# Layer 1 attention: ten chunks of probabilities turned by DMA, their low parts on GpSimd, and a second score pass on 64 rows

## The chip, the cores and the metric

The kernel runs on one core of one Trainium2 chip. A core has five engines with an instruction queue each: TensorE (PE in the profile; PEld are its weight loads), VectorE (DVE), ScalarE (ACT), GpSimd (POOL) and SyncE (SP), which issues most DMAs. On-chip data lies in SBUF, 128 partitions wide; TensorE writes to PSUM, eight banks of 128 x 512 numbers of 4 bytes. The metric is the device time of one execution in microseconds, the median of several runs.

## The reference, cut to what matters

A two-layer transformer backbone without a channel mixer, on 1024 latent tokens and 256 context tokens of width 1024, in 32-bit floats. Layer 0 mixes with multi-head latent attention. Layer 1, where the change lies, mixes with differential attention: eight heads, each with two score maps of head size 64 and one set of values of size 128.

```python
q = q.reshape(bsz, n, B_HEADS, 2, B_HEAD)              # 8 heads, 2 maps, 64
k = k.reshape(bsz, n, B_HEADS, 2, B_HEAD)
v = v.reshape(bsz, n, B_HEADS, 2 * B_HEAD)             # 128 per head
o1 = softmax(q[..., 0, :] @ [k, k_c][..., 0, :].T * scale) @ [v, v_c]
o2 = softmax(q[..., 1, :] @ [k, k_c][..., 1, :].T * scale) @ [v, v_c]
o = o1 - lam_full * o2
o = rms_norm(o, g_sub) * (1.0 - lambda_init)
x = layer_norm(ALPHA * x + gate * ((o * silu(gate_in)) @ out_w), ln_g, ln_b)
```

Queries and keys of the latent tokens are turned by axial rotary tables before this. Every query sees 1024 latent keys and 256 context keys, 1280 = ten chunks of 128. Layer 1 gives out the latent tokens alone.

## The kernel before, in words

**Precision.** TensorE works on 16-bit floats here. A number that must be more exact is split into a high part (its 16-bit rounding) and a low part (the rest, again 16 bits), and a product becomes three matmuls: high by high, high by low, low by high (`mm3`, L217 to L220).

**A tile of attention.** Layer 1 goes over 8 heads x 8 query tiles of 128 tokens, 64 tiles, in `attend` (L1789). For each tile and each map `m`:

- Scores (`chunk`, `sc_`, L1854 to L1868). A map's keys lie in `KS{m}`: the high part of its 64 rows on partitions 0 to 63, the low part on 64 to 127. Its queries lie in `QS{m}`, the high part twice, and in `Q1{m}`, the low part twice. The first pass (L1855) is QS by KS, which gives high by high and high by low at once; the second (L1856) is Q1 by KS. So 512 columns take two matmuls of 128 rows. The 1024 latent keys of a map fill two banks of kind `p` (four exist), the context keys of both maps share the one bank `c`.
- Maxima (`maxima`, L1870) on VectorE: per bank, then `bound{m}`, the negative maximum per query (L1879).
- Exponentials (`exps`, L1882) on ScalarE, with the bound as bias and the sum as a second result, into `p0` or `p1` in SBUF, 128 x 1280 in 32 bits.
- Join (`join`, L1889) on VectorE: `p0 + p1 * (-lambda * sum0 / sum1)`, 128 x 1280 (L1897).
- Turning: the weighted sum needs the probabilities with keys on the partitions, so each 128 x 128 chunk is transposed. Chunks 0 to 7 (`far`, L1900): ScalarE writes the high part, scaled by a power of two `lcf[0]` (L1902), VectorE the low part (L1903), into `dd`, and one transposing DMA moves both to `pd` (L1905). Chunks 8 and 9, the context (`turns`, L1791): TensorE transposes them in 32 bits (L1798), ScalarE takes the high part `ph` (L1803) and VectorE the low part `pl` (L1805) out of the bank.
- Weighted sum (`values`, L1809): 30 matmuls of 128 columns (L1820 to L1822), chunks 8 and 9 first. Then ScalarE scales it out (L1826) and squares it (L1827), GpSimd normalises it (L193, L194, L1838), and SP stores it. The unscaling of `lcf[0]` sits in `vic`, with which `w.us` scales each head's factor (L1613).

The weighted sum of a tile is written into the next tile's list of work (`before`).

**Beside it.** While the tiles of head h run, the weights of the next head are loaded, scaled and split (`weights`), and its keys, queries and values are projected (`keys`, `queries`, `vals`). Projections are TensorE's filler between scores and weighted sums. Keys and queries go through a rope (ScalarE L1643, VectorE L1645 and L1646, GpSimd L1647 and L1648), are split (high part on ScalarE, low part on GpSimd, L1666 and L1692), and are moved by DMAs of 64 partitions to the layout above (`k.move`, `q.move`, issued at L118): four DMAs per key chunk, eight per query block. Beside head 7 the output projection of finished tiles takes the place of the next head's projections (`out_tile`, L1952), after the output weights are prepared (`out_raw`, `out_split`).

**What sets the order.** Head 0's projections are written out in line (`prod_k1`, `prod_q1`, `prod_v1`, `prod_w`), and `lambda_of` works out lambda and `lcf` during layer 0's output projection. The rest of layer 1 goes through a planner, `Plan` (L688): every step is a task with an engine, a cost in us, what it reads and writes, and a due time `at` (in tiles) to which `OFF` adds an offset by kind. `run` simulates the engines greedily, with the rings of buffers (`TAG1`, `TAGL`, `PSB`), the windows `EPS1` and `AHEAD`, and `PORT`, the kinds that may not overlap on VectorE and GpSimd. The result is a fixed order of instructions on each engine (`tc.manual_schedule`). SP's queue is one of them: a DMA whose data are not ready holds up those behind it.

Of the kernel before, what the change touches and what calls it, by code (L numbers as in the profile page):

```python
# [46 lines left out]
OFF = {"bound0": -12.4, "bound1": -23.45, "exp0": -3.35, "exp1": -5.5, "far.hi": -26.55, "far.lo": -9.05,
       "far.move": -2.85, "g.add": -0.7, "g.bias": -0.45, "g.keep": -9.05, "g.load": -0.2, "g.sum": -1.65, "g.zero":
       1.4, "join": -11.0, "k.ctx": -17.05, "k.hi": 2.85, "k.lo": -1.45, "k.move": -17.4, "late": -57.8, "max.c":
       -5.8, "max0": -14.2, "max1": -5.85, "o.ga": -9.6, "o.gb": 2.3, "o.hi": 0.65, "o.lo": -25.2, "o.mul": -0.9,  # L50
       "open": -22.75, "prod": 0.2, "pv": -13.1, "pv.gate": -10.4, "pv.norm": 3.2, "pv.out": -6.5, "pv.sq": -25.1,
       "pv.store": -25.15, "pv.us": -11.45, "q.hi": -11.65, "q.lo": -8.45, "q.move": -9.9, "r.add": -10.4, "r.cos":
       0.1, "r.out": -0.95, "r.sin": -28.4, "r.swap": 2.65, "score0": 0.4, "score1": 0.1, "scorec": -4.45, "sums":
       -26.05, "turn.hi0": -0.35, "turn.lo0": 0.95, "turn0": -7.95, "v.gate": -5.1, "v.hi": -13.6, "v.keep": 3.6,
       "v.lo": -3.6, "v.octx": -38.95, "v.out": 2.9, "v.pctx": -0.05, "v.prod": -0.4, "v.silu": 0.25, "v.store":
       3.75, "v.turn": -4.5, "w.hi": 0.2, "w.lo": 0.05, "w.load": -5.55, "w.root": 1.6, "w.scale": 3.75, "w.sq":
       2.35, "w.sum": -21.8, "w.unit": 0.5, "w.us": -32.05, "x.gate": -13.35, "x.hi": -14.55, "x.lo": 4.2, "x.load":
       3.6, "x.low": 5.5, "x.mul": 0.8, "z.add": -9.0, "z.agg": -5.6, "z.bn": 3.65, "z.end": 16.45, "z.g": -11.3,
# [18 lines left out]
KD = 8  # L77
# [8 lines left out]
def hybrid_kernel(  # L86
# [601 lines left out]
    class Plan:  # L688
# [3 lines left out]
        PORT |= {("G", k) for k in "r.sin r.add k.lo q.lo v.lo o.lo x.gate x.lo z.mul z.g2 z.g3 s.lo v.sub".split()}  # L692
# [545 lines left out]
    def lambda_of():  # L1238
# [218 lines left out]
    def prod_k1(h, made=()):  # L1457
# [680 lines left out]
```

## Time and profile before

| what | value |
|---|---|
| median of 3 runs | 1667.47 us (1666.78 to 1668.52) |
| profiled execution, its own time | 1667.77 us |
| span of its instructions | 1666.0 us |
| granted TensorE clock, mean | 0.990 |
| layer 1 attention, first scores to last weighted sum | 918 to 1646 us |
| DMA, mean over the span | 113 GB/s |

The page gives busy times per engine over the whole span; a busy TensorE is one whose pipelined matmuls overlap without a gap, so the time of one more matmul is read from start to start and not from its duration. Waiting is told for each group as the idle time of its engine just before it, with the instruction that ended it. Views by stretch, by waits, by group and along the timeline answer for shorter times than the whole span.

### The profile page before, as it was taken

The numbers are of one execution on the slowest core, as the hardware profiler recorded it, in microseconds if no ns is written. First come the engines' busy times: TensorE is split into PE (matmuls) and PEld (weight loads), VectorE is DVE, ScalarE is ACT, GpSimd is POOL, SyncE is SP. The second block draws the span as 40 slices with busy tenths as digits, with TensorE's granted clock in tenths as the row PEclk, the third lists the DMA queues.
The fourth block names the chain that finished last, engine by engine and source line by source line (L and its number), as shares of the span: only waits on it lengthen the run. The fifth ranks groups of instructions, "written<-read, shape, count | busy, mean of one in ns | idle before, by whom it ended". The sixth has DMA issues, their size and how long they took to land. (4 is left out here: it accounts for less than half of the span.)

```text
span 1666.0 us, 35966 instructions
## 1 busy us (share of the span) xinstructions
PE 1586.8 (95%) x14052; PEld 1176.6 (71%) x14052; DVE 1241.7 (75%) x1941; ACT 1132.0 (68%) x2164; POOL 918.2 (55%) x772
## 2 busy tenths in 40 slices
PE   7999999999999999989999999999999999996998
PEld 6999966566666666667777586757576757675776
DVE  7757856777676676746773799999898979897764
ACT  2652147777887888945454888787878787868542
POOL 1523026767777777854555354545464646467554
PEclk9999999999999999989999999999999999998999
DMA  9347620101111111355442356554645444556562
GB/s 320 92 133 233 208 81 21 42 23 50 42 56 48 37 36 42 101 168 182 153 149 80 88 115 143 127 131 105 140 90 143 112 101 104 122 137 182 137 173 76
DMA packets 249463, 188.36 MB, mean 113 GB/s; under 512 B 147559, under 2 KB 224967, under 8 KB 249294
## 3 DMA queue, kind: packets, MB, share of 16 engines
q1 hardware_dynamic: 241422, 178.73, 40.3%
q10 hardware_dynamic: 7872, 7.34, 1.3%
q8 instruction: 110, 1.80, 0.5%
q14 instruction: 59, 0.48, 0.1%
HBM read 98.65 MB, written 27.07 MB: 75 GB/s over the span
## 5 line engine op out<-in xcount | busy, mean ns | idle before, releaser
L989 POOL TENSOR_TENSOR pl<-p,ph 128x1024 f16<-128x1024 f32 (+1 forms) x176 | 364.6, 2091 | 108.9 <-ACT ph L987 67.9
L985 ACT ACTIVATE p<-ps_a,esc 128x1024 f32<-128x1024 f32 (+1 forms) x176 | 188.6, 1072 | 63.9 <-PE ps_a L981 59.5
L934 DVE TENSOR_REDUCE mx<-ps_a 128x1 f32<-128x1024 f32 x128 | 156.3, 1222 | 75.7 <-PE ps_a L930 75.2
L1884 ACT ACTIVATE p<-ps_p,mx 128x512 f32<-128x512 f32 x256 | 174.4, 688 | 46.7 <-DVE mx L1879 44.6
L987 ACT CAST ph<-p 128x1024 f16<-128x1024 f32 (+1 forms) x176 | 176.5, 1006 | 4.8
L1877 DVE TENSOR_REDUCE mx<-ps_p 128x1 f32<-128x512 f32 x256 | 165.5, 680 | 8.1 <-PE ps_p L1856 7.9
L979 PE MATMUL ps_a<-qH,KH 100*128 100x512 f16 x320 | 122.5, 383 | 0.2 <-ACT p L985 0.2
L980 PE MATMUL ps_a<-qH,KL 96*128 96x512 f16 x320 | 121.9, 381 | 0.0
L981 PE MATMUL ps_a<-qL,KH 96*128 96x512 f16 x320 | 121.0, 378 | 0.0
L1897 DVE SCALAR_TENSOR_TENSOR p<-p,sm,p 128x1280 f32<-128x1280 f32 x64 | 107.4, 1678 | 1.2
L997 PE MATMUL ps_d<-Vh,ph 128*128 128x65 f16 x1344 | 105.1, 194 | 2.8 <-ACT ph L987 2.8
L998 PE MATMUL ps_d<-Vl,ph 128*128 128x64 f16 x1344 | 104.6, 194 | 0.0
L997 PEld LDWEIGHTS <-ph 128*128 128x128 f16 x1344 | 90.4, 98 | 14.4 <-issue 4.9
L1855 PE MATMUL ps_p<-KS,QS 128*128 128x512 f16 x256 | 97.7, 382 | 2.7 <-ACT p L1884 2.7
L1856 PE MATMUL ps_p<-KS,Q 128*128 128x512 f16 x256 | 97.3, 380 | 0.0
L1903 DVE SCALAR_TENSOR_TENSOR dd<-p,lcf,dd 128x1024 f16<-128x1024 f32 x64 | 88.9, 1390 | 5.8 <-ACT dd L1902 5.8
L998 PEld LDWEIGHTS <-ph 128*128 128x128 f16 x1344 | 87.9, 98 | 6.1
L1902 ACT ACTIVATE dd<-p,lcf 128x1024 f16<-128x1024 f32 x64 | 73.5, 1148 | 27.0 <-DVE p L1897 18.7
L1820 PE MATMUL ps_t<-vh,pd 128*128 128x128 f16 x512 | 91.3, 222 | 0.4 <-DMA pd<-dd 0.4
L1821 PE MATMUL ps_t<-vl,pd 128*128 128x128 f16 x512 | 91.3, 222 | 0.0
L1822 PE MATMUL ps_t<-vh,pd 128*128 128x128 f16 x512 | 91.3, 222 | 0.0
L193 POOL TENSOR_SCALAR ss<-ss 128x1 f32<-128x1 f32 x64 | 24.7, 385 | 96.2 <-ACT ps_t L1827 93.3
(503 smaller groups left out, 5387.7 us busy)
## 6 DMA issues: line engine op xcount, KB each, us to landing
ws<-in_dw SPq DMA_DIRECT2D x28, 512.0 KB, 5.2
adw<-in_ada_w SPq DMA_DIRECT2D x24, 512.0 KB, 4.8
adaw<-in_ada_w SPq DMA_DIRECT2D x16, 512.0 KB, 6.0
g<-sg_d SPq DMA_DIRECT2D x16, 512.0 KB, 4.0
sg_d<-gg ACTq DMA_DIRECT2D x40, 128.0 KB, 3.0
o_d<-op SPq DMA_DIRECT2D x7, 640.0 KB, 4.7
xt<-in_xT SPq DMA_DIRECT2D x16, 256.0 KB, 4.3
wgs<-in_w_in SPq DMA_DIRECT2D x32, 128.0 KB, 3.3
```

What stands on the lines that cost most here:

```text
L934: add("m.max", "D", 1.223, lambda t=t, ps=ps: dve.tensor_reduce(mx.tile[:, t, 0:1], ps.tile, axis=AX.X, op=ALU.max), r=[ps], w=[(mx, t)] i ...
L979: pe.matmul(s_, KH[i][:nr, ks], QH.tile[:nr, :], start=True, stop=False)
L980: pe.matmul(s_, KL[i][:DQ, ks], QH.tile[:DQ, :], start=False, stop=False)
L981: pe.matmul(s_, KH[i][:DQ, ks], QLo.tile[:DQ, :], start=False, stop=True)
L985: add("s.exp", "A", 1.114 if x else 0.682, lambda st=st, p32=p32: act.activation(p32.tile[:, :2 * n], st.tile[:, :2 * n], AF.Exp, scale=esc0),
L987: add("s.hi", "A", 1.046 if x else 0.618, lambda p32=p32, ph=ph: act.copy(ph.tile[:, :2 * n], p32.tile[:, :2 * n]), r=[p32], new=[ph], hol ...
L989: add("s.lo", "G", 2.14 if x else 1.17, lambda p32=p32, ph=ph, pl=pl: pool.tensor_tensor(pl.tile[:, :2 * n], p32.tile[:, :2 * n], ph.tile[ ...
L997: pe.matmul(v_()[:, t, :], w, Vh[:, k, h, :], start=(k == kcs[0] and t == 0), stop=False, skip_group_check=True)
L998: pe.matmul(v_()[:, t, :V0], w, Vl[:, k, h, :], start=False, stop=False, skip_group_check=True)
L1877: add(f"max{m}", "D", 0.68, lambda i=i, b_=b_: dve.tensor_reduce(mx.tile[:, 2 + 2 * m + i:3 + 2 * m + i], b_.tile, axis=AX.X, op=ALU.max, ...
L1884: add(f"exp{m}", "A", 0.78 if n == 512 else 0.57, lambda i=i, c0=c0, n=n, b=b, lo=lo: act.activation(p[m].tile[:, c0:c0 + n], b.tile[:, lo ...
L1897: add("join", "D", 1.55, lambda: dve.scalar_tensor_tensor(p[0].tile, p[1].tile, sm.tile[:, 4:5], p[0].tile, op0=ALU.mult, op1=ALU.add), r= ...
```

## The change

Four edits, and a new set of planner numbers.

1. All ten chunks go by DMA. `turns` is gone, with the two transposes per tile, `ph` and `pl`. ScalarE copies the whole of `p0` to a 16-bit `dh` (no scale), and GpSimd, no longer VectorE, subtracts to make `dl`. Each of the two has its own transposing DMA into `pd`, which now holds all ten chunks. The weighted sum takes the chunks in order.
2. The power-of-two scale moves into map 0's exponentials: `lcf[2]` holds the logarithm of `lcf[0]`, and a second small VectorE instruction adds it to `bound0`. The sum of map 0 carries the scale too, so `vic` is gone and `kci` takes its place.
3. The second score pass works on 64 rows. The queries' low part `QL` stays where GpSimd wrote it, map 0 on partitions 0 to 63 and map 1 on 64 to 127, and is not moved; that drops four of eight DMAs per query block. `KS1` is laid out the other way round (high part on 64 to 127), so that a map's high keys lie on the partitions of its low queries. The pass is four matmuls of 64 rows and 512 columns, in the order map 1, map 0, map 1, map 0. For the context, `kx` holds both maps' high keys on the diagonal and zeros elsewhere (cleared by GpSimd per head, two more DMAs), and one matmul of 128 rows and 512 columns serves both maps, ahead of two of 256 columns.
4. A tile's scores are one burst (`score.c`, `score0`, `score1`, `score.h`): the half passes of all four `p` banks come after the first passes of all four. In the plan, map 1's scores no longer come after map 0's exponentials.

```diff
-EPS1 = dict(P=0.05, A=0.0, D=0.15, G=0.15)
-AHEAD = 4.0
+EPS1 = dict(P=0.05, A=0.05, D=0.15, G=0.0)
+AHEAD = 6.75
...
-        PORT |= {("G", k) for k in "r.sin r.add k.lo q.lo v.lo o.lo x.gate x.lo z.mul z.g2 z.g3 s.lo v.sub".split()}
+        PORT |= {("G", k) for k in "r.sin r.add k.lo q.lo v.lo o.lo x.gate x.lo far.lo z.mul z.g2 z.g3 s.lo v.sub".split()}
...
-        dve.tensor_tensor(vic, kci, lcf[:, 1:2], op=ALU.mult)
+        act.activation(lcf[:, 2:3], lcf[:, 0:1], AF.Ln)
...
-            "pl": ([P, NT - KD, P], F16, 1), "dd": ([P, 2, KD * P], F16, 1), "pd": ([P, 2, KD, P], F16, 2),
+            "dh": ([P, NTOK], F16, 1), "dl": ([P, NTOK], F16, 1), "pd": ([P, 2, NT, P], F16, 2),
...
+            add("k.zero", "G", 0.45, lambda: pool.memset(ks[2].tile, 0.0), r=[PRJ], new=[ks[2]], at=at(0))
...
                     for m in range(2):
-                        r = slice(m * HD, m * HD + HD)
-                        dmv(ks[m].tile[:HD, c], H.tile[r, :n])
-                        dmv(ks[m].tile[HD:, c], L.tile[r, :n])
+                        r, o = slice(m * HD, m * HD + HD), slice(HD - m * HD, 2 * HD - m * HD)
+                        dmv(ks[m].tile[r, c], H.tile[r, :n])
+                        dmv(ks[m].tile[o, c], L.tile[r, :n])
+                        if c.start == SEQ:
+                            dmv(ks[2].tile[r, m * CTX:(m + 1) * CTX], H.tile[r, :n])
...
-                    dmv(q1[m].tile[:HD, c], L.tile[r, :])
-                    dmv(q1[m].tile[HD:, c], L.tile[r, :])
...
-            def sc_(out, m, c0, n):
-                pe.matmul(out, qs[m].tile[:, ts], ks[m].tile[:, c0:c0 + n], start=True, stop=False)
-                pe.matmul(out, q1[m].tile[:, ts], ks[m].tile[:, c0:c0 + n], start=False, stop=True)
...
+                def open_():
+                    pe.matmul(bc.tile, q1.tile[:, ts], ks[2].tile, start=True, stop=False, skip_group_check=True)
+                    for m in range(2):
+                        pe.matmul(bc.tile[:, m * CTX:(m + 1) * CTX], qs[m].tile[:, ts], ks[m].tile[:, SEQ:], start=False, stop=True, skip_group_check=True)
+                def part(m):
+                    for c0 in (0, 512):
+                        pe.matmul(st[c0, (m,)].tile, qs[m].tile[:, ts], ks[m].tile[:, c0:c0 + 512], start=True, stop=False, skip_group_check=True)
+                def halves_():
+                    for c0 in (0, 512):
+                        for m in (1, 0):
+                            r = slice(m * HD, m * HD + HD)
+                            pe.matmul(st[c0, (m,)].tile, q1.tile[r, ts], ks[m].tile[r, c0:c0 + 512], start=False, stop=True, skip_group_check=True)
...
+                add("score.h", "P", 2 * C(512) + 0.184, halves_, r=[(q1, qb)], w=ps_, at=a + 0.02)
...
+                    if m == 0:
+                        dve.tensor_scalar(mx.tile[:, 6:7], mx.tile[:, 6:7], lcf[:, 2:3], None, op0=ALU.add)
...
-                add("far.hi", "A", 1.24, lambda: act.activation(dd.tile[:, 0, :], p[0].tile[:, :KD * P], AF.Copy, scale=lcf[:, 0:1]), r=[p[0]], new=[dd], hold=1.15, at=g + PR["fa"])
+                add("far.hi", "A", 1.39, lambda: act.copy(dh.tile, p[0].tile), r=[p[0]], new=[dh], hold=1.3, at=g + PR["fa"])
+                add("far.lo", "G", 2.63, lambda: pool.tensor_tensor(dl.tile, p[0].tile, dh.tile, op=ALU.subtract),
+                    r=[p[0], dh], new=[dl], at=g + PR["fa"] + 0.05)
+                for i, d in enumerate((dh, dl)):
+                    add(f"far.move{i}", "S", 3.4, lambda i=i, d=d: sp.dma_start_transpose(pd.tile[:, i], d.tile),
+                        r=[d], w=[(pd, i)] if i else [], new=[] if i else [pd], hold=1.4, at=g + PR["fa"] + 0.1)
```

The offsets in `OFF` are new throughout; head 0's functions written out in line change in the same way as `keys` and `queries`.

More of the change, by code (lines that the diff above doesn't have):

```diff
@@ L43 @@
 PR = dict(s0=0.0, mx=0.1, ex=0.2, t0=0.15, t1=0.4, s1=0.3, pv=0.7, jo=0.6, fa=0.75)
-EPS1 = dict(P=0.05, A=0.0, D=0.15, G=0.15)
-AHEAD = 4.0
+EPS1 = dict(P=0.05, A=0.05, D=0.15, G=0.0)
+AHEAD = 6.75
 SP0, SP1, SP2 = 0.0, 0.3, 3.3
[L47 to L58, printed above, removed]
[3 rows of a table removed]
@@ new lines @@
+OFF = {"bound0": -19.65, "bound1": -12.9, "exp0": -6.3, "exp1": -13.85, "far.hi": -37.95, "far.lo": -0.55,
+       "far.move0": -25.3, "far.move1": -3.65, "g.add": -4.4, "g.bias": 6.05, "g.keep": -21.5, "g.sum": -3.25,
+       "g.zero": 3.35, "join": -13.4, "k.ctx": -11.45, "k.hi": -4.2, "k.lo": -0.15, "k.move": -3.9, "k.zero": -1.5,
+       "late": -101.2, "max.c": -3.0, "max0": -46.65, "max1": -8.1, "o.ga": -9.05, "o.gb": -1.9, "o.hi": -4.75,
+       "o.lo": -27.5, "o.load": -0.05, "o.mul": -4.5, "open": -19.7, "prod": -0.15, "pv": -18.45, "pv.gate": -11.85,
+       "pv.norm": 4.95, "pv.out": -10.2, "pv.sq": -11.55, "pv.store": -18.1, "pv.us": -14.1, "q.hi": -9.5, "q.lo":
+       6.2, "q.move": -28.5, "r.add": 2.7, "r.cos": 2.1, "r.out": -2.45, "r.sin": -19.05, "r.swap": 1.9, "score.h":
+       -18.15, "score0": -0.25, "sums": -21.5, "v.gate": -19.15, "v.hi": -30.9, "v.keep": 3.75, "v.lo": -10.6,
+       "v.octx": -56.25, "v.out": -7.65, "v.pctx": 0.3, "v.prod": -0.5, "v.silu": -15.45, "v.store": -13.95,
+       "v.turn": -2.35, "w.hi": -3.7, "w.lo": -1.75, "w.load": -2.95, "w.root": 5.5, "w.scale": 1.2, "w.sq": 6.5,
+       "w.sum": -54.95, "w.unit": 0.7, "w.us": -38.3, "x.gate": 2.9, "x.hi": -16.1, "x.lo": 8.3, "x.load": -16.5,
+       "x.low": -24.7, "x.mul": -3.5, "z.add": -33.95, "z.agg": 8.4, "z.end": -6.0, "z.g": -35.25, "z.g2": -4.8,
+       "z.g3": -6.25, "z.hi0": -29.15, "z.hi4": -0.6, "z.hi7": -34.05, "z.id": -16.95, "z.lo0": -21.45, "z.lo4":
+       -47.4, "z.lo7": -8.9, "z.mean": -5.25, "z.mm0": 3.7, "z.mm1": 3.3, "z.mul": 2.35, "z.o": -10.5, "z.out": 0.3,
+       "z.res": 1.35, "z.rstd": -9.0, "z.turn0": 1.05, "z.turn4": -1.75, "z.turn7": -2.95}
@@ L76 @@
 PW = 16.0
-KD = 8
 SWAP16 = [(i + 16) % 32 for i in range(32)]
@@ L1458, in prod_k1 @@
         kr = w1("kr")
-        kt1[h] = ks = [w1(f"KS{m}") for m in range(2)]
+        kt1[h] = ks = [*(w1(f"KS{m}") for m in range(2)), w1("kx")]
+        pool.memset(ks[2], 0.0)
         def fin(c, n):
@@ L1612, in weights @@
             if which:
-                add("w.us", "G", 0.2, lambda: pool.tensor_tensor(E_.tile, u.tile[:, 0:1], vic, op=ALU.mult), r=[u], new=[E_], at=at(0.6))
+                add("w.us", "G", 0.2, lambda: pool.tensor_tensor(E_.tile, u.tile[:, 0:1], kci, op=ALU.mult), r=[u], new=[E_], at=at(0.6))
                 USB[h], UNB[h] = E_, u
@@ L1686, in queries @@
             if b == 0:
-                QB[h] = [new1(f"Q1{m}") for m in range(2)], [new1(f"QS{m}") for m in range(2)]
+                QB[h] = new1("QL"), [new1(f"QS{m}") for m in range(2)]
             q1, qs = QB[h]
@@ L1698, in move @@
                     dmv(qs[m].tile[HD:, c], H.tile[r, :])
[L1699 to L1703 removed]
+            add("q.lo", "G", 1.16, low, r=[H, rr, PRJ], w=[(q1, b)] if b else [], new=[] if b else [q1], at=at(1) + 0.6)
+            add("q.move", "S", 6.30, move, r=[H, PRJ], w=[(x, b) for x in qs] if b else [], new=[] if b else qs, hold=4.60, at=at(1) + 0.7)
         def vals(h, g0, span):
```

118 lines of the change are left out of this document (43 added, 75 removed), and 3 rows, old and new, of the table OFF.

## The prediction

> **What bounds the kernel now.** I read the page's head and its busy times first, then the busy times by stretch, then who waited for whom, then the groups by line, then single stretches of the timeline. Page, head and part 1:
>
> ```profile
> span 1666.0 us, 35966 instructions
> PE 1586.8 (95%) x14052; PEld 1176.6 (71%) x14052; DVE 1241.7 (75%) x1941; ACT 1132.0 (68%) x2164; POOL 918.2 (55%) x772
> ```
>
> The change touches layer 1's attention. Its scores run from about 918 us on and its last weighted sum ends at 1646. Busy time by stretch (columns: stretch, length, then busy time of PE, PEld, DVE, ACT and POOL, granted clock, DMA share, GB/s):
>
> ```profile
> 915.00:1646.00 731.00, 693.98 (x5642) 502.98 (x5639) 627.00 (x1102) 558.58 (x1380) 385.63 (x427) 0.99 0.53 125
> 1009.00:1100.00 91.00, 87.13 (x730) 61.29 (x729) 86.05 (x148) 75.12 (x186) 41.99 (x55) 1.00 0.58 136
> 1500.00:1540.00 40.00, 26.38 (x208) 19.91 (x205) 31.49 (x46) 33.29 (x78) 30.46 (x21) 0.87 0.66 178
> ```
>
> TensorE is busy for 693.98 of 731.00 us, so the stage is TensorE's own work plus 37.0 us of waiting. In a middle head VectorE is nearly as full (86.05 of 91), ScalarE follows (75.12), and GpSimd has room (41.99). One spot differs: from 1500 to 1540, where the projections of the last head are done and the output projection has not begun, TensorE idles 13.6 us. What TensorE waits for, in the waits (total, times, longest) and in the groups (last number: idle before):
>
> ```profile
> PE ps_t L1820 <- DVE pl L1805: 19.6, 16, 5.8
> ...
> PE ps_p L1855 <- ACT p L1884: 2.7, 4, 2.1
> ```
>
> ```profile
> L1820 PE MATMUL ps_t<-vh,pd 128*128 128x128 f16 x512 | 91.3, 222 | 0.4 <-DMA pd<-dd 0.4
> L1820 PE MATMUL ps_t<-vh,ph 128*128 128x128 f16 x128 | 25.1, 221 | 23.0 <-DVE pl L1805 19.6 <-DVE uw L333 2.6 <-ACT p L1884 0.4
> L1798 PE MATMUL ps_t<-idr,p 128*128 128x128 f32 x128 | 24.8, 276 | 2.1 <-ACT ps_t L1827 1.4 <-DVE wy L1970 0.7
> ```
>
> 25.1 of the 37.0 us stand before the two turned chunks: 23.0 where a tile's weighted sum waits for their low part, 2.1 before their transposes. The eight chunks that come by DMA cost 0.4. Two of the waits lie in the spot without other work:
>
> ```profile
> 1509.89 0.24 PE L1820 MATMUL ps_t<-vh,ph 128*128 128x128 f16 x1 [4.29 <-DVE pl L1805]
> ...
> 1522.67 0.27 PE L1820 MATMUL ps_t<-vh,ph 128*128 128x128 f16 x1 [5.81 <-DVE pl L1805]
> ```
>
> **Part by part: TensorE.** Matmuls are pipelined, so I price them from start to start (timeline: start, duration):
>
> ```profile
> 1155.74 0.38 PE L1798 MATMUL ps_t<-idr,p 128*128 128x128 f32 x2
> 1155.96 0.27 PE L218 MATMUL ps_s<-wy,h1H 128*128 128x256 f16 x1
> ...
> 1157.38 0.38 PE L1855 MATMUL ps_p<-KS,QS 128*128 128x512 f16 x1
> 1157.60 0.38 PE L1856 MATMUL ps_p<-KS,Q 128*128 128x512 f16 x1
> 1157.81 0.38 PE L1855 MATMUL ps_p<-KS,QS 128*128 128x512 f16 x1
> ```
>
> (1) Two transposes take 1155.96 - 1155.74 = 0.22 us of TensorE. All 64 pairs go: 64 x 0.22 = 14.1 us.
>
> (2) The second score pass is four 512-column matmuls per tile at 0.215 (1157.38 to 1157.81 is two), 0.86 us. It becomes four on 64 rows. Fewer rows alone do not shorten a matmul; layer 0 has some on 96:
>
> ```profile
> L981 PE MATMUL ps_a<-qL,KH 96*128 96x512 f16 x320 | 121.0, 378 | 0.0
> L1856 PE MATMUL ps_p<-KS,Q 128*128 128x512 f16 x256 | 97.3, 380 | 0.0
> ```
>
> 378 against 380 ns. So there is a gain only if the two halves run side by side, map 1 on rows 64 to 127 and map 0 on rows 0 to 63. They read different rows and write different banks, and each pair stands together in the order; no row of this trace shows two matmuls in the array at once. If they do, two go for the price of one: 0.43 us a tile, 64 x 0.43 = 27.5 us. Going over to half rows and back is not in the trace either. Its lower end is nothing; its upper end is that the array runs empty on the way in and out, each time the 0.38 - 0.215 = 0.165 us that a matmul outlasts its turn, 0.33 together. I take the middle, 0.165 a tile, as nothing in the trace is nearer to one end: 64 x (0.43 - 0.165) = 17.0 us gained, bounds 6.4 and 27.5.
>
> (3) The context scores change from four 256-column matmuls to one of 512 and two of 256: the same columns, no change. The weighted sum keeps its 30 matmuls.
>
> **The other engines, per tile** (groups, mean ns):
>
> ```profile
> L1902 ACT ACTIVATE dd<-p,lcf 128x1024 f16<-128x1024 f32 x64 | 73.5, 1148 | 27.0 <-DVE p L1897 18.7 <-DMA pd<-dd 6.3 <-issue 2.0
> L1803 ACT ACTIVATE ph<-ps_t,lcf 128x256 f16<-128x256 f32 x64 | 30.3, 474 | 22.3 <-PE ps_t L1798 22.3
> L1748 ACT CAST vh<-Vf 128x1280 f16<-128x1280 f32 x7 | 8.8, 1255 | 0.0
> L1903 DVE SCALAR_TENSOR_TENSOR dd<-p,lcf,dd 128x1024 f16<-128x1024 f32 x64 | 88.9, 1390 | 5.8 <-ACT dd L1902 5.8
> L1805 DVE SCALAR_TENSOR_TENSOR pl<-ps_t,lcf,ph 128x256 f16<-128x256 f32 x64 | 30.5, 476 | 8.9 <-ACT ph L1803 8.9
> L1879 DVE TENSOR_SCALAR mx<-mx 128x1 f32<-128x1 f32 x128 | 34.9, 273 | 4.6
> L1749 POOL TENSOR_TENSOR vl<-Vf,vh 128x1280 f16<-128x1280 f32 x7 | 20.0, 2852 | 11.3 <-ACT vh L1748 11.3
> ```
>
> ScalarE loses 1.148 + 0.474 and gains 1.255, the copy of the same form and size in L1748: -0.37. VectorE loses 1.390 + 0.476 and gains one small operation, 0.273 (the guard added to map 0's bound): -1.59. GpSimd gains 2.852, the price of the same subtraction in L1749. Over 64 tiles VectorE goes from 627 to 525 us, ScalarE from 559 to 535, GpSimd from 386 to 568. The stage is to last some 690, so none of them becomes its bound, and TensorE's shorter work counts in full. The guard lies on the path from scores to exponentials; TensorE's other work covers it, as the wait for banks freed by the exponentials was 2.7 us in all. Without that cover it costs 64 x 0.273 = 17.5 us.
>
> **Waits that go, and that come.** The 25.1 us go with the low parts of L1805 and with L1798. The 10.1 us (4.29 + 5.81) at the spot without other work I don't count: there something else of the same tile is late next, the scores or the transposed chunks. That leaves 15.0. What comes: a tile's four score banks must now all be free before its half passes, and its maxima wait for these; I double the 2.7, so +2.7. In 1500 to 1540 GpSimd had 30.46 of 40; four tiles' low parts add 4 x 2.852 = 11.4, which makes 41.9, so +1.9. Net 15.0 - 4.6 = 10.4, bounds 0 and 25.1.
>
> The weighted sum now waits for the DMA alone. How much room that has, in a middle tile and in the transposing DMA's own row (issue time min/median/max, then landing):
>
> ```profile
> 1373.38 1.28 DVE L1903 SCALAR_TENSOR_TENSOR dd<-p,lcf,dd 128x1024 f16<-128x1024 f32 x1
> ```
>
> ```profile
> 1375.90 1.68 SPq L1905 DMA_TRANSPOSE pd<-dd  x1
> ```
>
> ```profile
> 1386.68 0.22 PE L1820 MATMUL ps_t<-vh,ph 128*128 128x128 f16 x1
> ```
>
> ```profile
> L1905 SPq DMA_TRANSPOSE pd<-dd x64: 1525/1856/4422, 933.3 to 1636.1; - x64
> ...
> DMA to landing us min/median/max: 4.2/4.3/6.4
> ```
>
> Landed at 1375.90 + 4.3 = 1380.2, read from 1386.68: 6.5 us of room. Copy plus subtraction take 1.255 + 2.852 in place of 1.148 + 1.390, 1.57 later, and that fits. On SP the low part's DMA waits for GpSimd, with the moves of the next keys and queries, the stores and the weight loads queued behind it; SP waits there for VectorE already. SP's issuing: 64 moves of query low parts go, two context moves per head come, and a tile's transposing DMA becomes two of 1280 columns.
>
> ```profile
> L118 SPq DMA_DIRECT2D Q<-kL x64: 461/594/1924, 890.3 to 1491.8; - x64
> ```
>
> That is 64 x 0.594 = 38 us less and 16 x 0.594 = 9.5 more; the two DMAs cost between 0.46 (by columns, 2 x 1.856 x 1280/2048 - 1.856) and 1.86 us more per tile, 30 to 119 in all. I take the near end: about even. The far end, spread over 731 us, is hidden while the room above lasts. The transposed bytes grow by a quarter, beside a DMA share of 0.53 in the stage. The context keys are cleared on GpSimd once per head, and ScalarE takes one logarithm ahead of the layer:
>
> ```profile
> L1884 ACT ACT_TABLE_LOAD x8 | 10.3, 1283 | 0.1
> ...
> L2010 POOL MEMSET gate<- 128x1024 f32 x1 | 1.0, 952 | 0.0
> ```
>
> TensorE's projections cover both, so I count nothing; uncovered they cost at most 8 x 0.952 and two table loads of 1.283, 10.2 us.
>
> **Sum.** 14.1 + 17.0 + 10.4 = 41.5 us. The profiled execution took 1667.77 us (span 1666.0), which becomes 1626.3; the median of the three runs is 0.30 lower, so 1626.0.
>
> **Rivals.**
> (B) The array empties fully both ways: 0.165 more per tile, 10.6 us, 1636.6. The Trainium skill's page TensorEngine Tiling (Array Packing), section Key Properties, says that a change of tiling mode drains TensorE; no run here shows it yet. By that rule the time is 1636.6.
> (C) Slower: the low parts are late out of GpSimd's queue. Ahead of one there may stand a rope and a normalisation:
>
> ```profile
> L194 POOL TENSOR_TENSOR ss<-ss,neghalf 128x1 f32<-128x1 f32 x63 | 45.8, 728 | 5.2
> L1647 POOL TENSOR_TENSOR rsw<-rsw,sinB 128x512 f32<-128x512 f32 x28 | 44.6, 1592 | 42.8 <-DVE rsw L1645 35.6 <-DVE sm L1892 7.3
> L1838 POOL TENSOR_SCALAR o<-o,ss 128x128 f32<-128x128 f32 x56 | 42.3, 755 | 5.8
> ...
> L193 POOL TENSOR_SCALAR ss<-ss 128x1 f32<-128x1 f32 x63 | 24.5, 388 | 94.1 <-ACT ps_t L1827 91.3
> ...
> L1666 POOL TENSOR_TENSOR kL<-kr,kH 128x512 f16<-128x512 f32 x14 | 20.0, 1428 | 12.0 <-ACT kH L1665 12.0
> ...
> L1648 POOL TENSOR_TENSOR kr<-kr,rsw 128x512 f32<-128x512 f32 x14 | 17.8, 1269 | 7.4 <-DVE kr L1646 6.6
> ```
>
> 1.592 + 1.269 + 1.428 + 0.388 + 0.728 + 0.755 = 6.2, and with the 1.57 this is 7.7 against 6.5 us of room: 1.2 late. In the 28 tiles with a rope that is 33.6 us, and the 15.0 are not won back: 1626.0 + 48.6 = 1674.6. It decides once waits on the low part reach about 40 us. For it: GpSimd's operations come in bunches. Against it: the order is planned anew, and the sum can be put later.
> (D) The halves do not run side by side, so the change does not do what it says: instead of 17.0 gained, 64 x 0.33 = 21.1 lost, 1664.1. For it: the 96-row line. Against it: disjoint rows and banks. The same section of the Trainium skill says that different tiles of the array can run matmuls in parallel; by that D falls away, and no run here shows it yet.
>
> **How the numbers follow.** Forecast 0.57, B 0.21, C 0.14, D 0.08. The forecast's own range is 1667.5 - 14.1 - 27.5 - 25.1 = 1600.8 to 1626.0 + 10.4 = 1636.4, and B with no waits won back ends at 1647.0. With a few us for the DMA terms, 1600 to 1651 leaves out C, D and little else, 0.2. A measurement of this kernel can tell about 0.2%, 3.3 us, from no change: faster 0.84 (the forecast and B but for their edges, a part of D and C), within it 0.05 (D's 1664.1 lies at the edge), slower 0.11 (most of C).
>
> **What would show it.** Right: no L1798 transposes; the four half passes of a tile take about 0.6 us from the first start to the next full matmul; the stage's TensorE idle time falls below 30 us; GpSimd near 570 us and VectorE near 525 in the stage. B: about 0.76 us for the four. D: 1.2. C: the weighted sum's first matmul waits, tile after tile, for the transposing DMA, and the DMA for GpSimd. Wrong altogether: TensorE's idle time grows by more than its work shrinks, or VectorE's join grows long beside the new subtraction.

## The result and the profile after

The changed kernel took 1638.38 us in the median (1634.76 to 1639.85, four runs), the kernel before beside it 1667.6 us: a ratio of 0.9819 [0.9806, 0.9832], 29.2 us faster. Measured once more, as the control of later experiments, it took 1640.5 us against 1667.06, a ratio of 0.984 [0.9826, 0.9853]. The profiled execution took 1634.76 us, 33.0 less than the profiled execution of before. The page's head and its line for TensorE:

```profile
span 1633.0 us, 35585 instructions
PE 1557.2 (95%) x13860; PEld 1132.1 (69%) x13860; DVE 1163.3 (71%) x1876; ACT 1111.0 (68%) x2102; POOL 1098.8 (67%) x844
```

Attention now ends earlier than before and other work of the layer comes after it, so a stretch that ends with the last weighted sum no longer compares like with like. I take each kernel from the same matmul, shortly ahead of attention, to its end: in the kernel before these are its last 5693 matmuls, in the changed kernel its last 5501, which lack 128 transposes and 64 context matmuls. That matmul ends at about 915.0 us before and at 911.6 after. In the control, the same program run again, it ends at 916.3, so the 3.4 us won ahead of it are scatter as far as these profiles tell. The other 29.6 of the 33.0 can be taken apart. Busy times by stretch, first of before, then of the changed kernel (there also the spot without other work, which has moved):

```profile
915.00:1666.00 751.00, 705.91 (x5693) 512.42 (x5690) 634.85 (x1116) 560.86 (x1385) 393.86 (x436) 0.99 0.52 123
```

```profile
911.58:1633.00 721.42, 680.29 (x5501) 469.57 (x5498) 557.64 (x1052) 538.46 (x1321) 573.28 (x506) 0.99 0.60 136
1470.00:1510.00 40.00, 27.74 (x229) 18.10 (x226) 30.47 (x49) 31.82 (x73) 34.17 (x26) 0.87 0.64 157
```

The reader subtracts the second number from the first: TensorE's busy time fell by 705.91 - 680.29 = 25.6 us, its idle time from 45.1 to 41.1, by 4.0. Together they make the 29.6. The control's profile, shown further down, has 679.64 us busy and 41.6 idle for the same matmuls, and the run without the guard's addition, where TensorE does the same work in the same order, 684.24 and 42.4; so such a busy time is known to some 5 us and the split to no better. VectorE lost 77.2 us, ScalarE 22.4, and GpSimd gained 179.4. What TensorE waits for in the changed kernel, and the groups that matter:

```profile
PE ps_p L1846 <- ACT p L1879: 17.8, 22, 5.4
PE ps_t L1803 <- DMA pd<-dl: 7.8, 10, 2.1
```

```profile
L1898 POOL TENSOR_TENSOR dl<-p,dh 128x1280 f16<-128x1280 f32 x64 | 169.5, 2648 | 49.6 <-ACT dh L1897 42.3 <-DMA pd<-dl 7.3
L1879 ACT ACTIVATE p<-ps_p,mx 128x512 f32<-128x512 f32 x256 | 173.9, 685 | 14.1 <-DVE mx L1873 13.6
L1897 ACT CAST dh<-p 128x1280 f16<-128x1280 f32 x64 | 80.4, 1257 | 60.6 <-DVE p L1892 52.9 <-POOL mv L1982 2.4 <-DMA pd<-dh 1.8
```

The waits for VectorE's low part (L1805 of before) and before the transposes are gone with these operations. Two others stand in their place: the first score pass (L1846) waits for exponentials to free its banks, 17.8 us where the kernel before had 2.7, and the weighted sum's low-part matmul (L1803) waits for the second transposing DMA, 7.8 us. A tile's scores along the timeline (start, duration):

```profile
1195.90 0.38 PE L1842 MATMUL ps_c<-KS,QS 128*128 128x256 f16 x2
1196.12 0.60 PE L1846 MATMUL ps_p<-KS,QS 128*128 128x512 f16 x2
1196.65 0.61 PE L1852 MATMUL ps_p<-KS,QL 64*128 64x512 f16 x4
1197.18 0.28 PE L217 MATMUL ps_s<-wx,h1H 128*128 128x256 f16 x1
```

From the first half pass to the next full matmul it is 1197.18 - 1196.65 = 0.53 us for four matmuls of 512 columns. In the starts of all 64 tiles in the trace, the two halves of a pair begin 3 ns apart and the second pair 223 ns after the first. The last full matmul before them takes 311 ns to the first half, the last half 308 ns to the next full matmul, where 216 is usual: about 0.19 us a tile for both changes of row mode.

### The profile page after: what moved, and what is told of

Its sections match the earlier page's. It is cut to its first block, busy times and chain, and to the rows that moved or that the text cites. A ratio compares the mean times of both kernels' runs of the same rounds, so it can differ in the third digit from the quotient of the medians.

```text
span 1633.0 us, 35585 instructions
## 1 busy us (share of the span) xinstructions
PE 1557.2 (95%) x13860; PEld 1132.1 (69%) x13860; DVE 1163.3 (71%) x1876; ACT 1111.0 (68%) x2102; POOL 1098.8 (67%) x844
## 4 chain that ended last, share of the span: by engine, by line
PE 61%; DVE 13%; ACT 10%; POOL 8%; DMA 5%; issue 3%; SPq 0%; POOLq 0%; DVEq 0%; ACTq 0%
ACT p L1879 5%; PE ps_a L978 4%; PE ps_a L979 4%; PE ps_a L980 4%; PE ps_s L217 4%; PE ps_s L219 4%; PE ps_s L218 4%; PE ps_a L929 3%; PE ps_a L217 3%; PE ps_a L219 3%; PE ps_a L218 3%; PE ps_d L1003 2%; PE ps_d L996 2%; PE ps_d L997 2%; POOL dl L1898 2%
## 5 line engine op out<-in xcount | busy, mean ns | idle before, releaser
L1898 POOL TENSOR_TENSOR dl<-p,dh 128x1280 f16<-128x1280 f32 x64 | 169.5, 2648 | 49.6 <-ACT dh L1897 42.3
L1879 ACT ACTIVATE p<-ps_p,mx 128x512 f32<-128x512 f32 x256 | 173.9, 685 | 14.1 <-DVE mx L1873 13.6
L1897 ACT CAST dh<-p 128x1280 f16<-128x1280 f32 x64 | 80.4, 1257 | 60.6 <-DVE p L1892 52.9
L1803 PE MATMUL ps_t<-vh,pd 128*128 128x128 f16 x640 | 111.0, 220 | 8.1 <-DMA pd<-dl 7.8
L1801 PE MATMUL ps_t<-vh,pd 128*128 128x128 f16 x640 | 111.8, 220 | 2.4 <-DVE wy L1957 1.7
L1802 PE MATMUL ps_t<-vl,pd 128*128 128x128 f16 x640 | 111.7, 220 | 0.0
L1892 DVE SCALAR_TENSOR_TENSOR p<-p,sm,p 128x1280 f32<-128x1280 f32 x64 | 103.5, 1617 | 4.0
L996 PEld LDWEIGHTS <-ph 128*128 128x128 f16 x1344 | 90.4, 98 | 14.2 <-issue 4.7
L1846 PE MATMUL ps_p<-KS,QS 128*128 128x512 f16 x256 | 79.0, 383 | 18.9 <-ACT p L1879 17.8
L929 PE MATMUL ps_a<-KH,qH 96*128 96x512 f16 x256 | 76.1, 379 | 0.9 <-ACT op L831 0.4
L1887 DVE TENSOR_REDUCE sm<-sm 128x2 f32<-128x6 f32 x64 | 10.0, 157 | 92.7 <-ACT p L1879 92.7
```

The source lines that it names most:

```text
L996: pe.matmul(v_()[:, t, :], w, Vh[:, k, h, :], start=(k == kcs[0] and t == 0), stop=False, skip_group_check=True)
L1879: add(f"exp{m}", "A", 0.78 if n == 512 else 0.57, lambda i=i, c0=c0, n=n, b=b, lo=lo: act.activation(p[m].tile[:, c0:c0 + n], b.tile[:, lo ...
L1898: add("far.lo", "G", 2.63, lambda: pool.tensor_tensor(dl.tile, p[0].tile, dh.tile, op=ALU.subtract), r=[p[0], dh], new=[dl], at=g + PR["fa ...
```

## The experiments

My theory after this result: TensorE's own work shrank as worked out, 14.1 us for the transposes and 14.7 for the half passes (28.8 together, where the busy times show 25.6 to 26.3), and the waits that went were nearly all replaced. The rivals: the halves or the burst did something else than counted (then undoing them alone should show another sum); or the new order of the plan, which the diff brings as a table of offsets, makes the gain.

**The second pass on full rows, order kept.**

```diff
-                            r = slice(m * HD, m * HD + HD)
-                            pe.matmul(st[c0, (m,)].tile, q1.tile[r, ts], ks[m].tile[r, c0:c0 + 512], start=False, stop=True, skip_group_check=True)
+                            pe.matmul(st[c0, (m,)].tile, q1.tile[:, ts], ks[m].tile[:, c0:c0 + 512], start=False, stop=True, skip_group_check=True)
```

The added rows put products of the other map's low query part with this map's low keys into the scores.

> The change with one thing undone: the second score pass uses all 128 rows again (the queries' low parts of both maps against a map's keys; the extra products are low by low and too small to count), in the same order of instructions. Theory T, TensorE's own work decides the time: in the changed kernel's trace the four half passes take 0.63 us a tile from the last first pass to the next full matmul, beyond the one matmul before them; four whole ones take 0.86. So 64 x 0.23 = 14.8 us more than the changed kernel's 1638.4: 1653. Rival R, the exponentials' chain decides and TensorE's work is partly hidden behind it: half of that or less, 1646 or below.

Measured: 1643.34 us (1642.94 to 1647.03), ratio 0.9857 [0.9843, 0.9871]. One tile, the busy times to the end, and the waits:

```profile
1194.12 1.03 PE L1851 MATMUL ps_p<-KS,QL 128*128 128x512 f16 x4
1194.98 0.38 PE L1840 MATMUL ps_c<-kx,QL 128*128 128x512 f16 x1
```

```profile
916.70:1645.20 728.50, 693.89 (x5501) 494.05 (x5498) 557.31 (x1052) 538.65 (x1321) 573.94 (x506) 0.98 0.60 134
```

```profile
PE ps_p L1846 <- ACT p L1878: 15.0, 18, 5.1
PE ps_t L1803 <- DMA pd<-dl: 5.9, 9, 1.8
```

Four full passes take 0.86 us (1194.12 to 1194.98) against 0.53. In work the halves are worth what the starts say: the control's 679.64 us busy are 14.2 less than the 693.89 here. In time they are worth 3 to 5 us by the medians (7.2 between these two profiles, from the same matmul), because TensorE's idle time is 34.6 us here and 41.6 in the control. So work that is taken out of the score burst comes back in good part as waiting: in the control 2.8 us more for the exponentials (17.8) and 3.1 more for the low part's DMA (9.0). That is the rival that I had called R.

**The halves of one map after the other.**

```diff
-                    for c0 in (0, 512):
-                        for m in (1, 0):
+                    for m in (1, 0):
+                        for c0 in (0, 512):
```

> The half passes in the order map 1, map 1, map 0, map 0, all else as in the changed kernel; same work, same order of everything else. Theory T, two of them run side by side only where they stand next to each other with different rows: one pair is left in place of two, so one more 0.215 us per tile, 13.8 us, 1652; the trace shows starts 3 ns apart once per tile, not twice. Rival, the array takes any of them as they come, or the pairs never truly overlapped: no change, 1638. A second rival, each step to other rows empties the array: the steps fall from three to one, which would give back some 0.1 us each, 1640.

Measured: 1643.59 us (1638.16 to 1645.23), ratio 0.9857 [0.9842, 0.9871]. The profiled execution, 1638.16, was the fastest of the four.

```profile
1199.60 0.59 PE L1846 MATMUL ps_p<-KS,QS 128*128 128x512 f16 x2
1200.13 0.61 PE L1852 MATMUL ps_p<-KS,QL 64*128 64x512 f16 x4
1200.67 0.28 PE L217 MATMUL ps_s<-wx,h1H 128*128 128x256 f16 x1
```

I had thought that without its neighbour on the other rows a half could not pair up. It does: four halves take 0.54 us again. In the starts, the first two begin 7 ns apart, the third 220 ns after the second, and the fourth 7 ns after the third. Each half of the rows seems to start when its own rows are free, though this order alone does not prove how, and the trace does not name the map of a half. The 3 to 5 us in the median are not explained: the pace of the halves is the same.

**All low-part matmuls at the end of the weighted sum, order kept.**

```diff
-                        for kc in (i0, i0 + 1):
-                            a, b = pd.tile[:, 0, kc, :], pd.tile[:, 1, kc, :]
-                            pe.matmul(pt.tile[:, :P], a, vh.tile[:, kc, :], start=kc == 0, stop=False)
-                            pe.matmul(pt.tile[:, :P], a, vl.tile[:, kc, :], start=False, stop=False)
-                            pe.matmul(pt.tile[:, :P], b, vh.tile[:, kc, :], start=False, stop=kc == NT - 1)
+                        todo = [(0, kc, v) for kc in range(NT) for v in (vh, vl)] + [(1, kc, vh) for kc in range(NT)]
+                        for x in range(3 * i0, 3 * i0 + 6):
+                            a, kc, v = todo[x]
+                            pe.matmul(pt.tile[:, :P], pd.tile[:, a, kc, :], v.tile[:, kc, :], start=x == 0, stop=x == 3 * NT - 1)
```

> The changed kernel with the 30 matmuls of a weighted sum in another order: the 20 with the high parts of all ten chunks first, the 10 with the low parts last; the plan and the order of all else are kept. Theory T: TensorE waits 7.8 us in all inside the weighted sum for the low part's transposing DMA, because the third matmul already reads it; with 20 matmuls of 0.056 us ahead of it these waits go: 6 to 8 us faster, 1631 to 1633. Rival: the time won is lost at the next wait, for the score banks that the exponentials free: 1637 to 1639 with longer waits there.

Measured: 1634.41 us (1631.08 to 1636.94), ratio 0.9797 [0.9782, 0.9812].

```profile
PE ps_p L1845 <- ACT p L1878: 19.7, 25, 5.5
...
PE ps_t L1802 <- DMA pd<-dl: 1.2, 2, 1.0
```

The wait for the low part's DMA fell from 7.8 to 1.2, and the one for the banks rose from 17.8 to 19.7. Of these 6.6 us 4 to 6 arrive by the medians. But the four runs reach up to 1636.94 and the changed kernel's down to 1634.76, and from the same matmul on this profile is only 1.5 to 1.7 us shorter than the two of the changed kernel. A gain is likely, its size is open. By its median this is the fastest version seen.

**No burst, scores of the two maps apart, on full rows.**

```diff
-                ps_ = [new1("p") for _ in range(4)]
...
-                def part(m):
-                def halves_():
+            def chunk(c0, m, a):
+                b = st[c0, (m,)] = new1("p")
+                def f():
+                    pe.matmul(b.tile, qs[m].tile[:, ts], ks[m].tile[:, c0:c0 + 512], start=True, stop=False, skip_group_check=True)
+                    pe.matmul(b.tile, q1.tile[:, ts], ks[m].tile[:, c0:c0 + 512], start=False, stop=True, skip_group_check=True)
...
+            for c0 in (0, 512):
+                chunk(c0, 0, g + PR["s0"] + 0.01)
```

> The changed kernel without the burst: each score bank gets its first and its second pass together, map 1's after map 0's exponentials in the plan, as before the change; for this the second pass has to use all 128 rows (as in the run with full rows). The plan is made anew with the changed kernel's offsets, which were not made for it. Theory T, the burst of four banks costs TensorE the longer waits for the exponentials (17.8 us against 2.7): 14.8 more for the full rows and 15 less waiting, 1634 to 1643. Rival, these waits come from ScalarE's and VectorE's order and not from the burst: as with full rows, 1653 or more, with the waits for the exponentials still there.

Measured: 1678.54 us (1674.29 to 1680.38), ratio 1.006 [1.0046, 1.0074].

```profile
PE ps_p L1847 <- ACT p L1871: 28.4, 17, 5.4
PE ps_t L1803 <- DMA pd<-dl: 10.4, 10, 2.3
```

The wait for banks grew to 28.4 us without the burst, so the burst as its cause is not borne out. But it took 35 us more than the full-row run, and it had to be planned anew, since its list of tasks differs. Whether the burst's absence or the new plan cost them needed a control. The next two runs are for that.

**The changed kernel with the old offsets.** The `OFF` table and `AHEAD = 4.0` of the kernel before (`far.move0` and `far.move1` get the old `far.move`); `EPS1` and every operation are the changed kernel's.

> The changed kernel with all its work, planned with the offsets and the look-ahead of the kernel before instead of its own; only the order differs. A (TensorE's work is worth 28.8 us whatever the order, the order sets the waits): TensorE's busy time in the stage stays near 665 us, the waits grow by 5 to 25 us, 1643 to 1663 us. B (the order is worth nothing, the loss without the burst was the burst's): within 3 us of the changed kernel's 1638.4.

**The full-row run, planned anew with its cost,** with the changed kernel's offsets:

```diff
-                add("score.h", "P", 2 * C(512) + 0.184, halves_, r=[(q1, qb)], w=ps_, at=a + 0.02)
+                add("score.h", "P", 4 * C(512), halves_, r=[(q1, qb)], w=ps_, at=a + 0.02)
```

> Burst, full second pass over 128 rows, and the order planned anew with that cost, with the changed kernel's offsets. It is the control for the run without the burst. A (a plan whose offsets were not fitted to it costs 10 us and more): over 1652 us, and most of the 40 us that the run without the burst lost are the plan's. B (the burst is what spares TensorE the waits): within 4 us of the full-row run with the frozen order, 1643.3.

Measured: the old offsets 1667.76 us (1665.6 to 1673.54, 12 runs), ratio 1.0005 [0.9995, 1.0016]; the full-row run planned anew 1665.63 (1660.27 to 1668.83), ratio 0.9986 [0.9973, 0.9998]. The old offsets' time lies above both ranges that I had put on it. Its busy times to the end, and its waits:

```profile
911.84:1664.20 752.36, 686.99 (x5501) 473.25 (x5498) 563.78 (x1052) 537.48 (x1321) 566.90 (x506) 0.98 0.57 130
```

```profile
PE ps_t L1803 <- DMA pd<-dl: 21.1, 15, 3.9
PE ps_c L1840 <- ACT p L1879: 17.9, 13, 3.4
PE ps_p L1846 <- ACT p L1879: 5.9, 12, 1.1
```

This is the sharpest finding of the study. All the work of the change is done, TensorE's count of matmuls is the changed kernel's, and the time is that of the kernel before. Idle time is 752.36 - 686.99 = 65.4 us, some 24 more than with its own offsets, and the busy time is 7 more, at a granted clock of 0.98. The full-row run with a plan of its own lost 22.3 us to the full-row run with the kept order, for the same instructions. So most of what the run without the burst lost can be the plan's; 12.9 us beyond the planned full-row run remain, less than new plans differ by, and the burst's own worth stays open.

**Two chunks turned by TensorE again,** on the old offsets: eight chunks by DMA, guard, burst and half passes stay.

```diff
+            def turns(state):
...
+                        pe.transpose(b.tile[:, j * P:(j + 1) * P], pc.tile[:, (8 + j) * P:(9 + j) * P], idn)
...
+                add("turn.hi0", "A", 0.46, lambda: act.copy(ph.tile, src()), r=[b], new=[ph], hold=0.37, at=g + PR["t0"] + 0.02)
+                add("turn.lo0", "D", 0.475, lambda: dve.tensor_tensor(pl.tile, src(), ph.tile, op=ALU.subtract), r=[b, ph], new=[pl], hold=0.385, at=g + PR["t0"] + 0.04)
```

> Order as in the run with the old offsets; two of the ten chunks are turned by TensorE again (two transposes, one copy by ScalarE and one subtraction by VectorE a tile), eight by DMA with the low part on GpSimd; burst, half passes and guard stay. A (the transposes cost TensorE 0.22 us a tile, and their waits come on top): 14.1 us of work more than the run with the old offsets, less the wait for the low part's DMA (7.8 us at most), plus 5 to 20 us of waits for the low part in VectorE: 11 to 30 us slower than that run. B (the ten-chunk transfers cost as much as they save): within 4 us of that run.

Measured: 1684.39 us (1680.79 to 1687.69), ratio 1.0098 [1.0083, 1.0113], 16.6 us slower than the run with the old offsets.

```profile
PE ps_t L1816 <- DVE pl L1803: 13.2, 11, 5.0
...
PE ps_t L1818 <- DMA pd<-dl: 4.8, 4, 1.4
```

```profile
915.23:1685.90 770.67, 705.27 (x5629) 492.41 (x5626) 582.40 (x1116) 547.24 (x1385) 531.10 (x506) 0.97 0.50 116
```

The kernel before's typical wait is back, and the DMA's has shrunk from 21.1 to 4.8. In sum the waiting is the same, 65.4 us idle in both runs. The busy time is 18.3 us more (705.27 against 686.99): 14.1 of it fit the transposes, and the rest came at a granted clock of 0.97 instead of 0.98. As this order is new too, and two plans can differ by more than 16.6 us, the run agrees with the price of the transposes and does not prove it.

**The low part on VectorE, planned anew, and with the order kept.** In the first, `far.lo` goes to VectorE in the plan with a cost of 1.62; in the second only the engine that does it changes, and on the other engines the order is the changed kernel's.

```diff
-                add("far.lo", "G", 2.63, lambda: pool.tensor_tensor(dl.tile, p[0].tile, dh.tile, op=ALU.subtract),
+                add("far.lo", "G", 2.63, lambda: dve.tensor_tensor(dl.tile, p[0].tile, dh.tile, op=ALU.subtract),
```

> The low part is subtracted by VectorE instead of GpSimd, planned anew. VectorE gets 64 subtractions of 1280 columns, some 1.5 us each, 96 us, and gives back up to 25 us on operations that ran longer beside GpSimd: 550 to 620-650 us in the stage. A (VectorE becomes the late one): waits of TensorE's score passes for the exponentials grow, 1645 to 1665 us. B (GpSimd's 2.65 us per low part and its effect on VectorE are the remaining cost): at or under 1636 us.

> The low part is subtracted by VectorE, with the changed kernel's order kept on every engine: the subtraction stands in VectorE's queue where it stood in GpSimd's plan. A (VectorE becomes the late one): VectorE's busy time in the stage grows from 550 to some 630 us, the maxima and with them the exponentials come later: 8 to 25 us slower than the control. B (the 50 us that the replanned form lost were its plan's): within 4 us of the control.

**Control, and the guard's addition left out.** The control is the changed kernel unaltered; in the other run the second instruction of `bound0` is gone, and the order is the same.

> The changed kernel once more, as the control of the three runs beside it: 1635 to 1641 us, 26 to 32 us faster than the kernel before.

> Leaves out the addition of the guard to map 0's bound (map 0's exponentials then lack their factor); every other instruction stands in the same order. A (the guard is covered, as forecast): within 2 us of the control. B (it lies on the way from the last maximum to the exponentials that free the score banks, of which TensorE waited 17.8 us in the profile): 64 times 0.214 us is 13.7 us at most, at the 22 tiles that waited 4.7 us: 4 to 14 us faster.

Measured: the low part on VectorE 1687.98 us planned anew (ratio 1.0119 [1.0101, 1.0138]) and 1681.18 with the order kept (1.0086 [1.0072, 1.01]); the control 1640.5; without the guard's addition 1640.85 (0.9835 [0.9819, 0.9851]). Busy times to the end of the control, then of the kept order with the low part on VectorE, with its waits and groups:

```profile
916.33:1637.60 721.27, 679.64 (x5501) 469.13 (x5498) 558.59 (x1052) 538.48 (x1321) 573.38 (x506) 0.99 0.60 136
```

```profile
913.81:1679.10 765.29, 697.75 (x5501) 474.01 (x5498) 629.33 (x1116) 539.77 (x1321) 420.15 (x442) 0.97 0.57 128
```

```profile
PE ps_p L1846 <- ACT p L1879: 35.8, 47, 3.9
PE ps_t L1803 <- DMA pd<-dl: 5.1, 5, 1.8
```

```profile
L1879 ACT ACTIVATE p<-ps_p,mx 128x512 f32<-128x512 f32 x256 | 174.4, 686 | 70.8 <-DVE mx L1871 33.4 <-DVE mx L1873 32.1 <-DVE uw L332 4.5
L1898 DVE TENSOR_TENSOR dl<-p,dh 128x1280 f16<-128x1280 f32 x64 | 111.0, 1735 | 4.2 <-DMA pd<-dl 3.5 <-ACT dh L1897 0.6
```

Planned anew, the time lies above both ranges that I had put on it, and part of it can be the plan's. With the kept order, which is the control's on the other engines, the 40.7 us come from the low part's place. A VectorE that is 70.7 us fuller (629.33 against 558.59) is still not full, yet ScalarE waits 65.5 us for the maxima and their bounds where the profile of the changed kernel had 13.6, and TensorE waits for the exponentials 47 times instead of 22. TensorE's idle time grows by 26 us, from 41.6 to 67.5, and its busy time for the same matmuls by 18. That is more than the 8 to 25 us that I had put on it. In this order, then, the subtraction's place on GpSimd is needed, which a count of TensorE's instructions does not show. Whether an order fitted to the low part on VectorE would lose as much, no run tells: the kernel before has its low parts there and waits 2.7 us for its score banks.

The guard's addition is covered. Without it ScalarE's wait falls from 13.6 to 10.7 us, and nothing arrives at the end. Its group, and the busy times to the end:

```profile
L1877 ACT ACTIVATE p<-ps_p,mx 128x512 f32<-128x512 f32 x256 | 173.9, 686 | 11.2 <-DVE mx L1871 10.7
```

```profile
913.25:1639.90 726.65, 684.24 (x5501) 472.51 (x5498) 547.16 (x988) 538.31 (x1321) 576.93 (x506) 0.98 0.60 135
```

**The kernel before, planned anew.** No work changes; the planner is told 0.05 us more for each score group.

```diff
-                x = add(f"score{m_}", "P", 2 * C(512), f, r=[(y[m], z) for m in ms for y, z in ((ks, c0), (qs, qb), (q1, qb))], new=[b], at=a)
+                x = add(f"score{m_}", "P", 2 * C(512) + 0.05, f, r=[(y[m], z) for m in ms for y, z in ((ks, c0), (qs, qb), (q1, qb))], new=[b], at=a)
```

> The kernel before with no change of work: its planner is told 0.05 us more for each of the five score groups of a tile, 0.25 us a tile as in the full-row run that was planned anew, so that the order comes out anew with offsets not fitted to it. A (a fitted order is worth some 20 us to either kernel, and the 22 to 29 us that the replanned forms of the changed kernel lost say nothing of its work): 10 to 30 us slower than before, 1678 to 1698 us. B (the kernel before bears a new order and the changed one does not: the new work left it less slack): within 5 us of before.

Measured: 1707.3 us (1705.3 to 1711.85), ratio 1.0243 [1.0227, 1.0259].

```profile
915.76:1710.00 794.24, 716.85 (x5693) 518.28 (x5690) 627.07 (x1116) 559.79 (x1385) 398.79 (x436) 0.97 0.50 117
```

```profile
PE ps_t L1820 <- DVE pl L1805: 27.8, 19, 5.4
PE ps_t L1820 <- DMA pd<-dd: 10.3, 7, 2.7
PE ps_t L1820 <- ACT p L1884: 8.5, 1, 8.5
```

An order that nobody fitted costs the kernel before 40 us, more than the 10 to 30 that I had put on it, with idle time up from 45.1 to 77.4, and the changed kernel 22 to 29. So both kernels stand on a fitted order, and the run with the old offsets doesn't say that the change is worth nothing: among the unfitted orders the changed work took 1667.8 us with the old offsets (1665.6 with full rows and its own) and the old work 1707.3. One order of each is too little to give that difference an interval. Nor does any run say what a better order of the old work would bring; with 705.91 us busy, only its 45.1 us of idle time were there to be won.

## Why the prediction was right, and where its steps were off

The forecast said 1626.0; the median was 12.4 above it and the profiled execution 8.5 above the 1626.3 made for it. The sign and the mechanism hold: of 31.1 us of TensorE's work 25.6 to 26.3 went by the busy times of the two profiles, 28.8 by the prices in the starts. Of the 10.4 us of waiting 3.5 to 4.0 went.

- **Step 1, the transposes:** 14.1 us forecast, from one pair. They are gone. Over all 64 pairs of the trace of before, the median from a pair's start to the next matmul is 218 ns, which makes 14.0. Busy time less the halves' 14.7 leaves 10.9 of the 25.6, known to some 5 us.
- **Step 2, the half passes:** 17.0 us forecast, 14.7 in the starts, 14.2 in the busy time against full rows. The halves run side by side, so rival D falls. Entering and leaving cost 95 + 92 ns a tile, where the term took 165 in all. The array does lose time both ways, as rival B had it, at about 0.095 us each instead of 0.165, so B's price was too high and the forecast's a little too low. The middle that the forecast took had no row behind it; the planner's own cost for this step, the 0.184 behind the `2 * C(512)` of `score.h` in the diff, lay nearer and was not used. The Trainium skill's page TensorEngine Tiling (Array Packing), section Key Properties, has both parts, tiles in parallel and a drain at a change of mode; the starts (3 ns apart, 311 and 308 ns against 216) agree with both.
- **Step 3, context scores:** no change forecast. From their first start to the next matmul they take 445 ns a tile against 437 in the median, 0.5 us in all.
- **The waits are the step that failed.** Net 10.4 us were to be won; idle time fell by 4.0 between the profiles, by 3.5 to the control's. The 19.6 us of waiting for VectorE's low part are gone. The other 5.5 of the 25.1 were read wrongly as part of it: the lines name other releasers (2.6 for `uw`, 1.4 for `ps_t`, 0.7 for `wy`, 0.4 for `p`, and the rest unnamed), and a wait of 1.7 us for `wy` stands before the weighted sum again. What came was put at 2.7 for the banks and 1.9 for the spot without other work; the banks' wait grew by 15.1 (2.7 to 17.8) and the weighted sum's wait for the low part's DMA was 7.8. Doubling a 2.7 us wait was no estimate for a burst that asks for four banks at once: the full-row run shows that this wait takes up part of any work saved in the burst. In the spot itself idle time stayed, 12.3 of 40 us after 13.6, as the forecast had it when it left the 10.1 us there out; the 1.9 that it added there do not show.
- **The low part's room:** 6.5 us of room against 1.57 later holds for most tiles, with 10 waits in 64. Rival C's mechanism is real in the trace, but at 7.8 us (9.0 in the control) instead of 48.6. The old offsets bring it to 21.1: whether C decides is a matter of the order.
- **The guard:** covered, as forecast; leaving it out changed nothing.
- **The other engines:** GpSimd and ScalarE came as forecast (179 us more with 182 forecast; 22 less with 24 forecast). VectorE lost 77 us instead of 102; some 19 of the missing 25 are the longer operations of the last section, the rest is not traced.
- **The transposing DMAs:** two of them issue in 1.35 us each, 2.70 a tile against 1.856, so 54 us more where the near end, 30, was taken. TensorE waited for these two DMAs 7.8 and 0.7 us; whether their issuing held up other DMAs was not looked at.

```profile
L1901 SPq DMA_TRANSPOSE pd<-dh x64: 1252/1348/4237, 928.9 to 1572.0; - x64
L1901 SPq DMA_TRANSPOSE pd<-dl x64: 1252/1350/3108, 931.6 to 1583.7; - x64
...
DMA to landing us min/median/max: 3.3/3.4/7.4
```

Of the signs that it named for being right, three came (no transposes, 0.53 us for the half passes, GpSimd at 573), and two did not: idle time stayed at 41 us instead of falling below 30, and VectorE at 558 instead of 525. The join did not grow, 1617 ns after 1678.

What the prediction did not weigh at all is the table of offsets. It priced the edits as if the order around them were as good as before, and that was so only because the change brought a fitted one.

## What to carry to other kernels

When a kernel's order is written by a planner, an edit and its plan are one change: try the edit once with the order frozen and once planned anew, and put the scatter of unfitted plans (here 22 to 40 us) beside any difference before believing it. When work is taken out of the bounding engine, price the wait in front of the place it is taken from: that wait can grow back unless the engine that ends it gets faster too, as half or more of the halves' work did here. An engine with a sixth of its time free can still be the late one (VectorE with the low parts, 629 of 765 us), so look at who waits for it and not at its share.

## What the runs showed of the hardware

Some of VectorE's float32 operations with two SBUF operands ran longer beside GpSimd's new subtraction. The weight scaling (13 instructions for each of two tiles) and the rope product, first of before, then of the changed kernel, then with the low part off GpSimd in the kept order:

```profile
L1623 DVE SCALAR_TENSOR_TENSOR wx<-ws,uw,wx 128x1024 f16<-128x1024 f32 x13 | 17.9, 1379 | 0.0
L1646 DVE TENSOR_TENSOR kr<-kr,cosB 128x512 f32<-128x512 f32 x14 | 9.7, 690 | 0.4
```

```profile
L1622 DVE SCALAR_TENSOR_TENSOR wx<-ws,uw,wx 128x1024 f16<-128x1024 f32 x13 | 24.8, 1904 | 1.1 <-ACT wx L1620 1.1
L1645 DVE TENSOR_TENSOR kr<-kr,cosB 128x512 f32<-128x512 f32 x14 | 15.2, 1087 | 0.3
```

```profile
L1622 DVE SCALAR_TENSOR_TENSOR wx<-ws,uw,wx 128x1024 f16<-128x1024 f32 x13 | 16.6, 1274 | 0.9 <-ACT wx L1620 0.9
L1645 DVE TENSOR_TENSOR kr<-kr,cosB 128x512 f32<-128x512 f32 x14 | 10.7, 764 | 0.3
```

1379 ns became 1904, and 1274 when the subtraction left GpSimd. Among the 13 of the changed kernel, the nine that overlap a subtraction in time took 2183 ns in the mean, and the four that overlap none 1269 to 1284. The second weight tile went from 1276 to 1816. The maxima that read from PSUM stayed at 680, beside a subtraction too, and the join, which has two SBUF operands but overlaps none of the 64 subtractions, did not grow. The Trainium skill's page SBUF — State Buffer, section "SBUF: two separate sides", says that a VectorE operation with two SBUF inputs and a GpSimd operation that reads SBUF hold a shared pair of ports in turn; the rows and the overlaps agree in direction.

More waiting came with slower work. In the kernel before, planned anew, idle time grew by 32 us and the busy time of the same matmuls by 10.9 (705.91 to 716.85, granted clock 0.99 to 0.97); with the low part on VectorE in the kept order, 26 us more idle came with 18.1 more busy (679.64 to 697.75, 0.99 to 0.97); with the old offsets, 24 with 7.3 (679.64 to 686.99, 0.99 to 0.98). These are beyond the 4.6 us by which runs with TensorE's order kept differ. The full-row run planned anew is not: 17 us more idle than with the kept order came with 2.8 more busy. Which way the cause runs, from the idle time to the clock or otherwise, no run here separates.
